# Turning x and the result in 32 x 32 blocks on VectorE instead of 128 x 128 tiles on TensorE

## The chip, the core and the metric

The kernel runs on one core of a Trainium2 chip. The metric is the device time of one execution in microseconds (us). The kernel before takes 1497.69 us, the median of 3 runs (1496.78 to 1500.61).

## What is computed

One layer of a streaming encoder, for 1024 prompt rows and 32 sample rows of 1024 features, all fp32. What matters here, cut from the reference:

```
h  = rms_norm(x, norm1_g) * (1 + sc1) + sh1
z  = h @ w_in                       # q, k, v, indexer, gMLP parts
attn = sparse attention over the top-k keys of each query; gm = gated MLP over chunks
y  = concat([attn, gm]) @ w_out
x  = x + g1 * y                     # x: the "residual"
h2 = rms_norm(x, norm2_g) * (1 + sc2) + sh2
x  = x + g2 * (square(relu(h2 @ w_ff1)) @ w_ff2)
return x, ...                       # y_prompt (1024 rows), y_sample (32 rows)
```

g1, g2, sc2 and sh2 have one value per feature, and differ between prompt and sample.

## The kernel before

From the product with w_out on, the kernel holds everything transposed: features on the 128 partitions, the 1056 rows (1024 prompt, then 32 sample) along the free dimension. A feature is then a partition, and the gates are one value per partition. The running x is kept in SBUF in eight blocks of 128 features, `xk(n, t0, n)`, each 128 x 1056; products are made in three chunks of 352 rows (`CW`, `NCK`). Each fp32 product is made of three passes over operands split in a high and a low part (`PASSES`), so a weight tile is first cast by ScalarE (L783) and its remainder taken by VectorE or GpSimd (L784).

Inputs and outputs in DRAM have rows of 1024 features, 4096 bytes. So x has to be turned twice:

- **In** (`x_col`, `x_chunk`, L755 to L769). For each feature block n, SyncE loads 128 columns of x into a buffer `xc` (two of them, tag XC): 1024 pieces of 512 bytes for the prompt and 32 for the sample. TensorE turns it in up to 128 x 128 tiles into PSUM (L768, 11 per block, the tiles being cut at the chunks' borders), and ScalarE copies each chunk to `xk` (L769). Blocks come in the groups (0, 1, 2), (3, 4), (5, 6, 7); for each group come x, then the weights (`wsplit`), then the products: for each chunk and block 24 matmuls (L839), whose sum VectorE multiplies by the gate and adds to `xk` in place (`gated`, L776). After the last group's chunk follows `norm2`.
- **Out** (`emit`, L867 to L882). The last part of `ff2` makes, for each feature block n and each chunk, 12 matmuls (L895) and adds the sum to `xk` (L776). When block n is done, TensorE turns it in nine tiles (L874), ScalarE copies them to a buffer `ot` (L876, L881), and SyncE stores it in pieces of 512 bytes (L879, L882). `ot` has one buffer for even n (tag OT) and shares the two buffers of XC for odd n. For the last block, n = 7, the store of the prompt is cut in two.

All transfers go through SyncE's queue, which issues them in order. The order of instructions on each engine is fixed when the kernel is built, by a planner that simulates a timeline; a buffer is given again when its last reader is done, for a store when it has landed.

Of the kernel before, what the change touches and what calls it, by code (L numbers as in the profile page):

```python
# [10 lines left out]
F32 = mybir.dt.float32  # L11
# [10 lines left out]
P = 128  # L22
D = 1024
KT = D // P
T = 1024
TS = 32
NT = T + TS
# [4 lines left out]
NB = T // P  # L32
# [6 lines left out]
CW = 352  # L39
NCK = 3  # L40
# [3 lines left out]
def blocks():  # L44
    return [(b, b * P, P) for b in range(NB)] + [(NB, T, TS)]
# [14 lines left out]
def hybrid_step(ctx: ExitStack, tc: tile.TileContext, i, o):  # L60
    nc = tc.nc
# [11 lines left out]
    def slot(shape, dt, name):  # L73
        return sp.tile(shape, dt, name=name, tag="S", bufs=15)
# [7 lines left out]
    def tp(name="tp"):  # L82
        return psz.tile([P, 512], F32, name=name, tag="C", bufs=2)
# [48 lines left out]
    ident = cst.tile([P, P], F32, name="ident")  # L132
# [71 lines left out]
    pt = tp("wst")  # L204
# [408 lines left out]
    key, c = {NB: sc_c[:, 384 + SD + 1024 + 256:].bitcast(I16)}, 0  # L613
# [112 lines left out]
    wf = phf.enter_context(tc.tile_pool(name="wf", bufs=1, reuse_waits="tile"))  # L726
    wn = phf.enter_context(tc.tile_pool(name="wn", bufs=1, reuse_waits="tile"))

    def mm(name="mm"):
        return psf.tile([P, 512], F32, name=name, tag="mm", bufs=6)  # L730
# [14 lines left out]
    def mix_at(k, c):  # L745
        return (gm[k - 4] if k >= 4 else attn[k])[:, :, c * CW:(c + 1) * CW]
# [3 lines left out]
    def xk(k, t0, n):  # L750
        if x2[k // 2] is None:
            x2[k // 2] = slot([P, 2, NT], F32, f"x2_{k}")
        return x2[k // 2][:, k % 2, t0:t0 + n]

    def x_col(n):  # L755

        x = wf.tile([P, NB + 1, P], F32, name="xc", tag="XC", bufs=2)
        nc.sync.dma_start(x[:, 0:NB, :], i["x_prompt"][0, :, n * P:(n + 1) * P].rearrange("(b p) c -> p b c", p=P))
        nc.sync.dma_start(x[:TS, NB, :], i["x_sample"][0, :, n * P:(n + 1) * P])
        return x  # L760

    def x_chunk(n, x, c):

        pt = tp("xt")
        for b, t0, m in blocks():
            a, e = max(t0, c * CW), min(t0 + m, (c + 1) * CW)
            if e > a:
                nc.tensor.transpose(pt[:, a - c * CW:e - c * CW], x[a - t0:e - t0, b, :], ident[a - t0:e - t0, a - t0:e - t0])  # L768
        nc.scalar.copy(xk(n, c * CW, CW), pt[:, :CW])  # L769


    def gated(part, k, c, ps):

        for s, a, n in spans(c):
            y = xk(k, c * CW + a, n)
            nc.vector.scalar_tensor_tensor(y, ps[:, a:a + n], mod[:, 8 * part + k, s:s + 1], y, op0=OP.mult, op1=OP.add)  # L776

    def wsplit(src, rearr, a, b, name, eng, extra=False):
        raw = rp.tile([P, a, b], F32, name=name + "r", tag="R4", bufs=2)
        nc.sync.dma_start(raw, src.rearrange(rearr, p=P))  # L780
        ws = wr.tile([P, 2, a, b], F32R, name=name, tag="E", bufs=1) if extra else wf.tile([P, 2, a, b], F32R, name=name, tag="W8", bufs=4)
        with tc.high_priority():
            nc.scalar.copy(ws[:, 0], raw)  # L783
        eng.tensor_tensor(ws[:, 1], raw, ws[:, 0].bitcast(F32), op=OP.subtract)  # L784
        return ws
# [8 lines left out]
    def norm2(c):  # L794

        acc = wn.tile([P, CW], F32, name="acc", tag="NA", bufs=3)
        for k in range(KT):
            x = xk(k, c * CW, CW)
            if k == 0:
                nc.scalar.activation(acc, x, AF.Square)  # L800
            else:
                sq = wn.tile([P, CW], F32, name="sq", tag="NS", bufs=3)
                nc.scalar.activation(sq, x, AF.Square)
                (nc.gpsimd if k < 7 else nc.vector).tensor_tensor(acc, acc, sq, op=OP.add)
        ps = tp("ssq")
        g = [(j, t, min(P, CW - t)) for j, t in enumerate(range(0, CW, P))]
        ms = small(4, "ms2")
        nc.gpsimd.memset(ms, 1.0)
        for j, t, m in g:
            nc.tensor.matmul(ps[:m, j:j + 1], acc[:, t:t + m], ones, start=True, stop=True)  # L810
        for j, t, m in g:
            nc.scalar.copy(ms[:m, j:j + 1], ps[:m, j:j + 1])
        r = rsqrt(ms, P, 4, "r2", D)
        y = tp("r2b")
        for j, t, m in g:
            nc.tensor.matmul(y[:, t:t + m], r[:m, j:j + 1].to_broadcast([m, P]), ident[:m, :m], start=True, stop=True)
        for k in range(KT):
            if (KT * c + k) % 3 == 0:
                h2.append(slot([P, 3, 2, CW], F32R, f"hh{c}_{k}"))
            hk = h2_at(k, c)  # L820
            f = wn.tile([P, CW], F32, name="hf2", tag="NH", bufs=2)
            for s, a, n in spans(c):
                nc.vector.scalar_tensor_tensor(f[:, a:a + n], xk(k, c * CW + a, n), a2[:, k, s:s + 1], y[:, a:a + n], op0=OP.mult, op1=OP.mult)
                nc.scalar.activation(hk[:, 0, a:a + n], f[:, a:a + n], AF.Identity, bias=mod[:, 24 + k, s:s + 1])
                nc.vector.scalar_tensor_tensor(hk[:, 1, a:a + n], f[:, a:a + n], mod[:, 24 + k, s:s + 1], hk[:, 0, a:a + n].bitcast(F32), op0=OP.add, op1=OP.subtract)  # L825

    KO = (4, 5, 6, 7, 0, 1, 2, 3)
    for ns in ((0, 1, 2), (3, 4), (5, 6, 7)):
        for n in ns:
            x = x_col(n)  # L830
            for c in range(NCK):
                x_chunk(n, x, c)
        ws = {n: wsplit(i["w_out"][0, :, n * P:(n + 1) * P], "(k p) c -> p k c", KT, P, "wo", nc.vector if n in (0, 2) else nc.gpsimd) for n in ns}
        for c in range(NCK):
            for n in ns:
                ps = mm("wo")
                for k in KO:
                    for q, (x, y) in enumerate(PASSES):
                        nc.tensor.matmul(ps[:, :CW], ws[n][:, x, k, :], mix_at(k, c)[:, y, :], start=k == KO[0] and q == 0, stop=k == KO[-1] and q == 2)  # L839
                gated(2, n, c, ps)  # L840
            if ns[-1] == KT - 1:
                norm2(c)
# [3 lines left out]
    NG = FF // (GH * P)  # L846
    phr.close()
    wr = phf.enter_context(tc.tile_pool(name="wr", bufs=1, side="right", reuse_waits="tile"))
# [15 lines left out]
                nc.gpsimd.tensor_tensor(hid[n][:, 1, c * CW:(c + 1) * CW], r, hi.bitcast(F32), op=OP.subtract)  # L864
        return hid

    def emit(n):  # L867

        ot = (wf if n % 2 else wr).tile([P, NB + 1, P], F32, name="ot", tag="XC" if n % 2 else "OT", bufs=2 if n % 2 else 1)
        for b0 in range(0, NB + 1, 4):  # L870
            pt = tp("yt")
            for b in range(b0, min(b0 + 4, NB + 1)):
                m = P if b < NB else TS
                nc.tensor.transpose(pt[:m, (b - b0) * P:(b - b0 + 1) * P], xk(n, b * P, m), ident)  # L874
            if b0 < NB:
                nc.scalar.copy(ot[:, b0:b0 + 4], pt.rearrange("p (b c) -> p b c", c=P))  # L876
                if n == KT - 1 or b0 == 4:
                    f0 = b0 if n == KT - 1 else 0
                    nc.sync.dma_start(o[0][0, f0 * P:(b0 + 4) * P, n * P:(n + 1) * P].rearrange("(b p) c -> p b c", p=P), ot[:, f0:b0 + 4])  # L879
            else:  # L880
                nc.scalar.copy(ot[:TS, NB, :], pt[:TS, :P])  # L881
                nc.sync.dma_start(o[1][0, :, n * P:(n + 1) * P], ot[:TS, NB, :])  # L882

    def ff2(gs):

        ks = [(g, k) for g in gs for k in range(GH)]
        for n4 in range(KT // 4):
            w = {g: wsplit(i["w_ff2"][0, g * GH * P:(g + 1) * GH * P, n4 * 512:(n4 + 1) * 512], "(k p) c -> p k c", GH, 512, "w2", nc.vector) for g in gs}
            for nn in range(4):
                n = 4 * n4 + nn  # L890
                for c in range(NCK):
                    ps = mm("f2")
                    for g, k in ks:
                        for q, (x, y) in enumerate(PASSES):
                            nc.tensor.matmul(ps[:, :CW], w[g][:, x, k, nn * P:(nn + 1) * P], hids[GH * g + k][:, y, c * CW:(c + 1) * CW], start=(g, k) == ks[0] and q == 0, stop=(g, k) == ks[-1] and q == 2)  # L895
                    gated(5, n, c, ps)
                if gs[-1] == NG - 1:
                    emit(n)

    hids = ff1((0, 1, 2))  # L900
    for g in range(NG - 1):
        if g:
            hids.update(ff1((2 * g + 2,)))
        if g < NG - 2:
            ff2([g])
        hids.update(ff1((2 * g + 3,)))
    ff2([NG - 2, NG - 1])
    phf.close()

# [35 lines left out]
```

## Time and profile before

| | us |
|---|---|
| median of 3 runs | 1497.69 |
| the profiled execution | 1491.26 |
| its span | 1489.5 |
| TensorE matmul busy in it | 1403.9 |
| VectorE / ScalarE / GpSimd busy | 821.7 / 549.2 / 551.0 |

The profile is of one execution, taken by the hardware profiler; times in it are from the start of its span. PE is TensorE's matmuls, PEld its weight loads, DVE VectorE, ACT ScalarE, POOL GpSimd, SP SyncE, which issues the transfers. The chain of waits is the work that ended last, followed back from the end: at each step to what released it.

### The profile page before, as it was taken

What the parts mean: (1) busy time and instruction counts of PE and PEld (TensorE: products, weight loads), DVE (VectorE), ACT (ScalarE), POOL (GpSimd) and SP (SyncE); (2) the same over time, 40 slices, a digit from 0 to 9 for tenths busy, and PEclk for the clock granted to TensorE, in tenths of its full rate; (3) what the DMA queues carried; (4) which work ended last, traced back from release to release, by engine and by line L of the source; (5) the groups of instructions that cost most, each with busy time, mean ns of one, the idle gap of its engine ahead of it and who ended that gap; (6) DMA issues with size and microseconds to landing.
All of it is one profiled execution on the core that took longest, in us unless ns stands there. A gap on an engine that the chain in (4) does not pass through costs nothing.

```text
span 1489.5 us, 23938 instructions
## 1 busy us (share of the span) xinstructions
PE 1403.9 (94%) x8952; PEld 1259.2 (85%) x8952; DVE 821.7 (55%) x1969; ACT 549.2 (37%) x1162; POOL 551.0 (37%) x831
## 2 busy tenths in 40 slices
PE   5889797887899999999999999999999999999998
PEld 1767576655567878899999999999999999999998
DVE  1689999998475867511673544335443344433422
ACT  2653356665545755522552212221122211122122
POOL 1646768667951433221342112221122211222120
PEclk9999899999899999999999999999999999999999
DMA  9221111256464221223111111111111111111113
GB/s 361 74 62 47 56 46 58 89 149 231 141 239 114 48 74 60 79 82 85 44 43 43 43 51 50 43 43 45 56 44 43 43 57 44 43 43 46 54 30 88
DMA packets 127611, 114.99 MB, mean 77 GB/s; under 512 B 24180, under 2 KB 95304, under 8 KB 126984
## 3 DMA queue, kind: packets, MB, share of 16 engines
q1 hardware_dynamic: 127496, 113.46, 24.8%
q8 instruction: 71, 1.16, 0.3%
q14 instruction: 44, 0.36, 0.1%
HBM read 97.97 MB, written 15.47 MB: 76 GB/s over the span
## 4 chain that ended last, share of the span: by engine, by line
PE 70%; DVE 16%; POOL 5%; issue 4%; ACT 3%; DMA 1%; SPq 0%; DVEq 0%; ACTq 0%; POOLq 0%
PE f L895 25%; PE f L858 23%; PE wo L839 6%; DVE tcjk L542 4%; PE pv L715 3%; PE lgp L690 3%; PE z L313 3%; PE ppt L702 3%; DVE tbjk L542 2%; PE xt L768 1%; POOL tasm L570 1%; DVE hh L825 1%; POOL wsp L195 1%; PE ada L154 1%; PE qst L360 1%
## 5 line engine op out<-in xcount | busy, mean ns | idle before, releaser
L895 PE MATMUL f<-hid,w 128*128 128x352 f32 x2304 | 377.3, 323 | 0.0
L858 PE MATMUL f<-hh,w 128*128 128x352 f32 x2304 | 372.3, 322 | 0.6 <-DVE hh L825 0.6
L858 PEld LDWEIGHTS f<-hh,w 128*128 128x128 f32 x2304 | 369.2, 188 | 0.9 <-DVE hh L825 0.9
L895 PEld LDWEIGHTS f<-hid,w 128*128 128x128 f32 x2304 | 369.3, 188 | 0.5
L776 DVE SCALAR_TENSOR_TENSOR x<-f,mod,x 128x352 f32<-128x352 f32 x480 | 222.4, 489 | 255.2 <-PE f L895 253.4
L313 PE MATMUL z<-wsp,h 128*128 128x512 f32 (+1 forms) x1152 | 284.9, 398 | 14.1 <-DVE ssh L424 4.6
L313 PEld LDWEIGHTS z<-wsp,h 128*128 128x128 f32 x1152 | 214.5, 198 | 72.2 <-issue 12.7
L863 POOL TENSOR_TENSOR rel<-rel 128x352 f32<-128x352 f32 x96 | 85.2, 889 | 512.6 <-ACT hid L862 512.6
L783 ACT CAST w<-w2r 128x1024 fp32r<-128x1024 f32 x32 | 33.6, 1049 | 285.7 <-PE f L895 272.7
L784 DVE TENSOR_TENSOR w<-w1r,w 128x1024 fp32r<-128x1024 f32 x32 | 40.6, 1267 | 138.0 <-ACT w L783 138.0
L860 ACT ACTIVATE rel<-f 128x352 f32<-128x352 f32 x96 | 44.3, 462 | 155.6 <-PE f L858 153.9
L864 POOL TENSOR_TENSOR hid<-rel,hid 128x352 fp32r<-128x352 f32 x96 | 91.3, 953 | 6.9
L695 POOL TENSOR_SCALAR lg<-lg,ast 128x128 f32<-128x128 f32 (+8 forms) x72 | 51.6, 719 | 97.1 <-DVE ast L694 73.9
L783 ACT CAST w<-w1r 128x1024 fp32r<-128x1024 f32 x32 | 33.5, 1047 | 85.7 <-PE f L858 73.3
L690 PE MATMUL lgp<-kst,qs 128*128 128x256 f32 (+1 forms) x336 | 61.0, 305 | 2.8 <-ACT qs L362 2.5
L195 POOL TENSOR_TENSOR wsp<-wraw,wsp 128x512 fp32r<-128x512 f32 (+1 forms) x44 | 55.0, 1262 | 16.9 <-ACT wsp L194 15.1
L784 DVE TENSOR_TENSOR w<-w2r,w 128x1024 fp32r<-128x1024 f32 x32 | 39.0, 1219 | 39.5 <-ACT w L783 39.5
L692 ACT ACTIVATE lg<-lg,ast 128x128 f32<-128x128 f32 (+8 forms) x72 | 53.9, 750 | 15.1 <-DVE ast L691 10.5
L542 DVE TENSOR_SCALAR_CACHE_REDUCE tcjk<-ya,tcsm 128x768 bf16<-128x768 int16 (+1 forms) x64 | 57.9, 942 | 0.9
L715 PE MATMUL pv<-pT,v 128*64 128x128 f32 (+2 forms) x624 | 57.7, 278 | 0.0
L776 DVE SCALAR_TENSOR_TENSOR x<-wo,mod,x 128x352 f32<-128x352 f32 (+2 forms) x32 | 15.1, 489 | 71.7 <-PE wo L839 71.7
L690 PEld LDWEIGHTS lgp<-kst,qs 128*128 128x128 f32 (+1 forms) x336 | 44.4, 186 | 11.1 <-issue 7.0
(349 smaller groups left out, 1839.5 us busy)
## 6 DMA issues: line engine op xcount, KB each, us to landing
wada<-in_w_ada_dram SPq DMA_DIRECT2D x24, 1024.0 KB, 6.0
w1r<-in_w_ff_dram SPq DMA_DIRECT2D x32, 512.0 KB, 4.0
w2r<-in_w_ff_dram SPq DMA_DIRECT2D x32, 512.0 KB, 3.8
wraw<-in_w_in_dram SPq DMA_DIRECT2D x40, 256.0 KB, 3.0
gm<-gmd SPq DMA_DIRECT2D x4, 1056.0 KB, 5.6
x<-in_x_prompt_dram SPq DMA_DIRECT2D x4, 1024.0 KB, 9.7
gmd<-gmt SPq DMA_DIRECT2D x8, 512.0 KB, 3.6
qn<-qd SPq DMA_DIRECT2D x8, 512.0 KB, 4.7
```

What stands on the lines that cost most here:

```text
L195: (nc.vector if c0 == CU and k % 2 else nc.gpsimd).tensor_tensor(ws[:, 1], raw, ws[:, 0].bitcast(F32), op=OP.subtract)
L313: nc.tensor.matmul(p[:m, :n], h[b][:, k, x, :], w[k][:, y, :], start=k == 0 and q == 0, stop=k == KT - 1 and q == 2)
L542: nc.vector.tensor_scalar(jk[:, :ncol[j]], src, val, None, op0=op, op1=OP.add, accum_out=cnt[:, j:j + 1])
L690: nc.tensor.matmul(ps[:m, d:d + kk.shape[1]], x, kk, start=q == 0, stop=q == 1)
L715: nc.tensor.matmul(ps[64 * j:64 * j + 64, :m], vv, pts[j][:w, k, :m], start=k == 0, stop=k == len(kts) - 1)
L776: nc.vector.scalar_tensor_tensor(y, ps[:, a:a + n], mod[:, 8 * part + k, s:s + 1], y, op0=OP.mult, op1=OP.add)
L784: eng.tensor_tensor(ws[:, 1], raw, ws[:, 0].bitcast(F32), op=OP.subtract)
L839: nc.tensor.matmul(ps[:, :CW], ws[n][:, x, k, :], mix_at(k, c)[:, y, :], start=k == KO[0] and q == 0, stop=k == KO[-1] and q == 2)
L858: nc.tensor.matmul(ps[:, :CW], ws[n][:, x, k, :], h2_at(k, c)[:, y, :], start=k == 0 and q == 0, stop=k == KT - 1 and q == 2)
L863: nc.gpsimd.tensor_tensor(r, r, r, op=OP.mult)
L864: nc.gpsimd.tensor_tensor(hid[n][:, 1, c * CW:(c + 1) * CW], r, hi.bitcast(F32), op=OP.subtract)
L895: nc.tensor.matmul(ps[:, :CW], w[g][:, x, k, nn * P:(nn + 1) * P], hids[GH * g + k][:, y, c * CW:(c + 1) * CW], start=(g, k) == ks[0] and ...
```

## The change

x and the result are turned by VectorE's transpose, which turns each 32 x 32 block of a tile in its place, and the transfers put the blocks where they belong. A quarter q of a feature block is 32 features on 32 partitions; a transfer places, for each group j of 32 rows, the 32 x 32 square of rows 32j to 32j+31 and the quarter's features, rows on partitions, in columns 32j to 32j+31. Each contiguous piece is 32 fp32, 128 bytes. One transpose of 128 x 1056 then gives the feature block. Per block there are 4 transfers for the prompt and 4 for the sample, in and out. The TensorE transposes and ScalarE copies of both places are dropped. Block n = 7 of the result is now turned and stored chunk by chunk, right after each chunk's sum; each of its three chunks takes a buffer of its own from tag XC.

```diff
--- before.py
+++ after.py
@@ -752,21 +752,20 @@
             x2[k // 2] = slot([P, 2, NT], F32, f"x2_{k}")
         return x2[k // 2][:, k % 2, t0:t0 + n]
 
-    def x_col(n):
-
-        x = wf.tile([P, NB + 1, P], F32, name="xc", tag="XC", bufs=2)
-        nc.sync.dma_start(x[:, 0:NB, :], i["x_prompt"][0, :, n * P:(n + 1) * P].rearrange("(b p) c -> p b c", p=P))
-        nc.sync.dma_start(x[:TS, NB, :], i["x_sample"][0, :, n * P:(n + 1) * P])
-        return x
-
-    def x_chunk(n, x, c):
-
-        pt = tp("xt")
-        for b, t0, m in blocks():
-            a, e = max(t0, c * CW), min(t0 + m, (c + 1) * CW)
-            if e > a:
-                nc.tensor.transpose(pt[:, a - c * CW:e - c * CW], x[a - t0:e - t0, b, :], ident[a - t0:e - t0, a - t0:e - t0])
-        nc.scalar.copy(xk(n, c * CW, CW), pt[:, :CW])
+    def squares(t, n):
+
+        return [t[:, n * P + 32 * q:n * P + 32 * q + 32].rearrange("(j a) b -> a j b", a=32) for q in range(4)]
+
+    def quarter(t, q):
+        return t[32 * q:32 * q + 32].rearrange("a (j b) -> a j b", b=32)
+
+    def x_rows(n):
+
+        x = wf.tile([P, NT], F32, name="xc", tag="XC", bufs=2)
+        for t, src in ((x[:, 0:T], i["x_prompt"][0]), (x[:, T:NT], i["x_sample"][0])):
+            for q, s in enumerate(squares(src, n)):
+                nc.sync.dma_start(quarter(t, q), s)
+        nc.vector.transpose(xk(n, 0, NT), x)
 
 
     def gated(part, k, c, ps):
@@ -827,9 +826,7 @@
     KO = (4, 5, 6, 7, 0, 1, 2, 3)
     for ns in ((0, 1, 2), (3, 4), (5, 6, 7)):
         for n in ns:
-            x = x_col(n)
-            for c in range(NCK):
-                x_chunk(n, x, c)
+            x_rows(n)
         ws = {n: wsplit(i["w_out"][0, :, n * P:(n + 1) * P], "(k p) c -> p k c", KT, P, "wo", nc.vector if n in (0, 2) else nc.gpsimd) for n in ns}
         for c in range(NCK):
             for n in ns:
@@ -864,22 +861,15 @@
                 nc.gpsimd.tensor_tensor(hid[n][:, 1, c * CW:(c + 1) * CW], r, hi.bitcast(F32), op=OP.subtract)
         return hid
 
-    def emit(n):
-
-        ot = (wf if n % 2 else wr).tile([P, NB + 1, P], F32, name="ot", tag="XC" if n % 2 else "OT", bufs=2 if n % 2 else 1)
-        for b0 in range(0, NB + 1, 4):
-            pt = tp("yt")
-            for b in range(b0, min(b0 + 4, NB + 1)):
-                m = P if b < NB else TS
-                nc.tensor.transpose(pt[:m, (b - b0) * P:(b - b0 + 1) * P], xk(n, b * P, m), ident)
-            if b0 < NB:
-                nc.scalar.copy(ot[:, b0:b0 + 4], pt.rearrange("p (b c) -> p b c", c=P))
-                if n == KT - 1 or b0 == 4:
-                    f0 = b0 if n == KT - 1 else 0
-                    nc.sync.dma_start(o[0][0, f0 * P:(b0 + 4) * P, n * P:(n + 1) * P].rearrange("(b p) c -> p b c", p=P), ot[:, f0:b0 + 4])
-            else:
-                nc.scalar.copy(ot[:TS, NB, :], pt[:TS, :P])
-                nc.sync.dma_start(o[1][0, :, n * P:(n + 1) * P], ot[:TS, NB, :])
+    def emit(n, c=None):
+
+        t0, t1 = (0, NT) if c is None else (c * CW, (c + 1) * CW)
+        ot = (wf if n % 2 else wr).tile([P, NT], F32, name="ot", tag="XC" if n % 2 else "OT", bufs=2 if n % 2 else 1)[:, :t1 - t0]
+        nc.vector.transpose(ot, xk(n, t0, t1 - t0))
+        parts = [(ot[:, :min(t1, T) - t0], o[0][0, t0:min(t1, T)])] + ([(ot[:, T - t0:], o[1][0])] if t1 > T else [])
+        for src, dst in parts:
+            for q, d in enumerate(squares(dst, n)):
+                nc.sync.dma_start(d, quarter(src, q))
 
     def ff2(gs):
 
@@ -894,7 +884,9 @@
                         for q, (x, y) in enumerate(PASSES):
                             nc.tensor.matmul(ps[:, :CW], w[g][:, x, k, nn * P:(nn + 1) * P], hids[GH * g + k][:, y, c * CW:(c + 1) * CW], start=(g, k) == ks[0] and q == 0, stop=(g, k) == ks[-1] and q == 2)
                     gated(5, n, c, ps)
-                if gs[-1] == NG - 1:
+                    if gs[-1] == NG - 1 and n == KT - 1:
+                        emit(n, c)
+                if gs[-1] == NG - 1 and n < KT - 1:
                     emit(n)
 
     hids = ff1((0, 1, 2))
```

## Rows read from the trace of the kernel before

**Rows 1.** The page: busy time of each engine; the chain's shares by engine

```profile
PE 1403.9 (94%) x8952; PEld 1259.2 (85%) x8952; DVE 821.7 (55%) x1969; ACT 549.2 (37%) x1162; POOL 551.0 (37%) x831
...
PE 70%; DVE 16%; POOL 5%; issue 4%; ACT 3%; DMA 1%; SPq 0%; DVEq 0%; ACTq 0%; POOLq 0%
```

**Rows 2.** Busy time by stretch: its ends and length, engines, clock, DMA share

```profile
core 0: us, PE busy (x) PEld busy (x) DVE busy (x) ACT busy (x) POOL busy (x), PEclk, DMA share, GB/s
623.70:713.40 89.70, 89.70 (x538) 82.08 (x538) 14.44 (x28) 23.51 (x46) 21.53 (x14) 1.00 0.32 90
713.40:765.40 52.00, 51.44 (x333) 51.15 (x331) 42.23 (x94) 30.20 (x71) 17.21 (x18) 1.00 0.14 41
765.40:1430.70 665.30, 665.25 (x4153) 665.25 (x4154) 274.46 (x506) 144.39 (x238) 168.81 (x184) 1.00 0.15 46
1430.70:1484.10 53.40, 53.40 (x354) 52.52 (x354) 15.39 (x31) 11.70 (x24) 1.86 (x2) 1.00 0.25 69
1484.10:1489.50 5.40, 1.29 (x9) 0.71 (x7) 0.71 (x2) 1.32 (x3) 0.00 (x0) 0.96 0.49 132
```

**Rows 3.** The chain from 620 to 720 us, in order: start, length, what

```profile
by line: PE wo L839 80.8%; PE xt L768 15.0%; PE pv L715 2.7%; PE ppt L702 1.2%; PE ssq L810 0.5%
...
623.77 1.20 PE xt L768 x7
...
712.14 0.75 PE xt L768 x4
```

**Rows 4.** The chain from 1430 to 1490 us

```profile
by line: PE f L895 77.3%; PE yt L874 12.4%; PE f L858 1.6%; ACT ot L876 1.0%; DVE x L776 0.9%; ACTq L941 0.2%; issue 0.2%
...
1437.12 0.22 PE yt L874 x2
...
1482.98 1.13 PE f L895 x7
...
1484.13 0.56 DVE x L776
...
1484.74 0.56 PE yt L874 x3
...
1485.32 0.58 ACT ot L876
```

**Rows 5.** VectorE on fp32 by shape, busy, mean ns; last min/median/max ns

```profile
L241 DVE TENSOR_SCALAR x<-x,rxy 128x1024 f32<-128x1024 f32 x8 | 6.8, 877 | 0.1
L784 DVE TENSOR_TENSOR w<-w1r,w 128x1024 fp32r<-128x1024 f32 x32 | 40.6, 1267 | 138.0 <-ACT w L783 138.0
L804 DVE TENSOR_TENSOR acc<-acc,sq x3: 510/519/524, 711.3 to 740.1; 128x352 f32<-128x352 f32 x3
```

**Rows 6.** DMA, 291 to 294 us, a 128-byte store (40 slices; packets, MB, share)

```profile
GB/s 0 0 0 0 0 0 0 0 0 0 0 0 0 0 0 0 0 0 75 123 109 109 109 109 109 108 109 109 109 109 109 109 109 108 24 0 0 0 0 0
...
q1 hardware_dynamic: 1040, 0.13, 33.6%
```

**Rows 7.** DMA, 1461 to 1467.75 us, a block's 512-byte store

```profile
q1 hardware_dynamic: 1088, 0.54, 29.0%
```

**Rows 8.** DMA, 520 to 540 us, a load in 256-byte pieces

```profile
q1 hardware_dynamic: 2064, 0.52, 11.7%
```

**Rows 9.** SyncE's issues in order of time: start, length, line, what

```profile
607.44 0.38 SPq L758 DMA_DIRECT2D xc<-in_x_prompt_dram  x1
...
608.95 0.84 SPq L759 DMA_DIRECT2D xc<-in_x_sample_dram  x1
...
623.77 2.61 SPq L780 DMA_DIRECT2D wor<-in_w_out_dram  x2
...
1486.40 0.50 SPq L882 DMA_DIRECT2D out_dram<-ot  x1
```

**Rows 10.** The sample's stores, L882: issue min/median/max ns; issue to landing

```profile
L882 SPq DMA_DIRECT2D out_dram<-ot x8: 332/332/570, 1443.8 to 1486.4; - x8
...
DMA to landing us min/median/max: 2.0/2.2/3.0
```

## The prediction

> **What bounds the kernel now.** Read the page's busy shares and chain of waits first: TensorE is busy for 94% of the span and holds 70% of the chain that ended last [rows 1]. The share is an average, so the next view is the table by stage [rows 2]. From 623.7 to 1484.1 us TensorE idles for 0.6 us altogether, nearly all of it in 713 to 765 us, while VectorE has 14.4 of 89.7 us, 42.2 of 52.0 us and 15.4 of 53.4 us of work in the three stages that the change touches or borders on. [...] Then the chain, cut to the two places: it runs through every transpose of x [rows 3] and through the transposes of the result [rows 4]. After the last matmul TensorE is done and the chain is VectorE, three transposes, a ScalarE copy and the stores: 5.4 us from 1484.1 to the end.
>
> **TensorE's transposes of x.** 88 transposes go, in 18 pieces of the chain, the first and the last of which stand in [rows 3]; the pieces add up to 15.0 us, the 15.0% that the head of this 100 us cut gives. Matmuls stand on both sides of each piece and wait for nothing, so all of it comes off: **-15.0 us**. The 24 ScalarE copies that go with them cover nothing and are worth nothing.
>
> What is late next? x must now be landed and turned by VectorE before the first product of that column block is added to it. Loads: per block 4 transfers of 1024 packets and 4 of 32, 264 packets per DMA engine instead of 66. No load of 128-byte packets is in the trace. The nearest row is a store of 1040 such packets: 131 KB at a flat 109 GB/s is 1.20 us, 18.8 ns a packet on each of 16 engines [rows 6]. The other bound is the 512-byte packet, 0.290 x 6.75 us x 16 / 1088 = 28.8 ns [rows 7]; a 256-byte load comes to 0.117 x 20 us x 16 / 2064 = 18.1 ns of engine time [rows 8]. I take 18.8: 5.0 us a block, at most 7.6. SyncE issues four transfers in 1.5 us, so 0.5 us apiece [rows 9]: 64 issues instead of 16, 32 us of queue in some 105 us. The first two blocks can start at 607.4 us, as now [rows 9], and are there at about 613.5 and 618.5 us (616 and 624 at the upper bound). A block's 24 matmuls of 161 ns [rows 4] take 3.9 us, so the first product is added at 627.6 us and the third block's at 635.4 us. The third block's load starts when the first has been turned (about 615 us) and is landed by 624, or 632 at the upper bound. All are in time.
>
> VectorE's transpose is not in the trace. From below: the 128 x 1024 scalar operation on fp32, 0.88 us. From above: one pass at 1.27 us for each of the four groups of 32 partitions, 5.1 us. By the nearest row, a 128 x 1024 two-input fp32 operation of 1.27 us [rows 5], 1056 columns take 1.3 us, which I take; 352 columns take 0.52 us, as in the 128 x 352 row [rows 5]. Eight times 1.3 is 10 us beside the 14.4 of 89.7 us, hidden; even 8 x 5.1 = 41 us fits there. [...]
>
> VectorE's queue is in order: behind a transpose that waits for its load stand attention's last evictions and the splits of w_out, and TensorE waits for those. Behind x's issues on SyncE stands the third w_out load, which goes out at 623.8 us when its buffer is free [rows 9]. If all is placed after the data this costs nothing; I take nothing and keep 8 us as the other end (rival 1).
>
> The stage from 713 to 765 us, where VectorE is nearly full, gets no new work: all eight blocks of x are turned before it. Its start moves up with TensorE's, so the 0.6 us idle stays.
>
> **TensorE's transposes of the result.** Seventy-two, 7.5 us of the chain in 30 pieces; the last 0.56 us comes after the last matmul [rows 4]. **-6.9 us** ahead of that point: the 53.4 us stage becomes 46.5, 5.8 us a block. Against it, per block: VectorE 15.4 / 8 + 1.3 = 3.2 us, 7.0 at the upper bound; SyncE 8 issues of 0.5 us, 4.0; the rings 264 x 18.8 ns = 5.0 us where now 66 packets at 28.8 ns need 1.9. All below 5.8, the rings with 14% to spare: **this is where the change can fail** (rival 2). An even block's buffer is needed again two blocks, 11.6 us, after its own transpose; its stores are landed after some 6 us.
>
> [...]
>
> **The end.** Times here are from the last matmul's end. Now: stores are issued until 1486.4, the last lands 2.2 us later, and 0.9 us follow to the span's end [rows 9, 10], +5.4. After: block 6 is added up at -5.8 + 0.6 and turned by -3.9; its 8 issues last to +0.1. Packets start 0.75 us after an issue and run from -3.15 to +1.8. Block 7 comes in three chunks. The first (352 columns, 88 packets an engine, 1.65 us) is issued to 2.1, moved by 3.5 and landed at 3.8; the second is issued to 4.1. The third has the first chunk's buffer (two of them, in turn), so its transpose waits for 3.8, not for its sum at 0.6, and ends at 4.35. Eight issues follow (four of the prompt, four of the sample); the last starts at 7.85, lands 2.2 us later and is followed by 0.9 us: +10.95. **+5.5 us**. Without the buffer's wait it would be 0.25 less, since SyncE is busy to 4.1 anyway. If the issues took the 0.33 us of the sample's store [rows 10] apiece, with no gap, some 1.2 us less.
>
> **Sum.** -15.0 - 6.9 + 5.5 = -16.4 us. The profiled execution took 1491.26 us (span 1489.5 and 1.8 around it), so 1474.9 for the same. The median of the runs is 1497.69, 6.4 us above that execution; the difference is carried over: **1481 us**, with its own range 1475 to 1488.
>
> **Rivals.**
> 1. *x or w_out come late at the start.* Place: SyncE's queue at 615 to 630 us. If the fifth block's x is put ahead of the third w_out load, its eight issues wait for a buffer and take 4 us themselves, and the load with its split is some 5 us late, once in the first group and at most once more: 3 to 8 us of TensorE idle, 1484 to 1489. For it: order on a queue is fixed beforehand, on guessed transfer times. Against it: x is first wanted a whole block later than now.
> 2. *The stores bind: slower.* Place: the rings from the first result on. Above 5.8 us / 264 = 22 ns a packet, each block's stores last longer than its matmuls, the buffers come back late and TensorE waits. The stores begin at -46.5 + 5.8 + 0.6 + 1.3 + 0.75 = -38 and need 8 x 264 packets, so the end is -36.8 + 2.11 per ns. At 28.8 ns that is +24, 18.6 above now's: 21.9 - 18.6 leaves 3.3 us, 1494. From 30.4 ns it is slower; at twice the row's price, 37.6 ns, the end is +42.5 and the time is 1497.7 + 15.2 = 1513. For it: the one row of 128 bytes is a single short store, from 128 partitions at a pitch of 4224 bytes, where this one reads 32 partitions and writes at 4096. Against it: the 512-byte stores now write at that very pitch at full rate.
> 3. *The first saving doesn't arrive.* If the VectorE work of 713 to 765 us stays where it is, only -6.9 + 5.5 = -1.4 is left: 1496. For it: 42 of 52 us busy there. Against it: that work hangs on sums that move up.
> 4. *VectorE binds.* At 5.1 us a transpose the result's stage needs 7.0 us a block, 1.2 x 8 us back and 1.2 more in the last chunk, 10.8: 1492.
>
> **How the numbers follow.** Forecast 60%; rival 1, 15%; rival 2 slower than before 9%, and in its part from 22 to 30 ns 6%; rival 3, 5%; rival 4, 3%; a reordering elsewhere 2%. Below 0.3%, 4.5 us, a measurement here can't tell a change from none. Faster by more than that: the forecast, rival 1, rival 4 and a part of rival 2's milder half, 80%. The same: the other part, rival 3 and some of the reordering, 10%. Slower: 10%. The range goes from 1474 (an end no longer than now gives 1476, and small gains between matmuls) to 1495, rival 2 at 28.8 ns.
>
> **What would show it.** Right: no transposes in the chain after 620 us; the products with w_out within 75 us in place of 89.7; the result's stage at 46.5 us with TensorE full; transposes of 1.3 us; 18 to 20 ns a packet; an end of some 11 us. Wrong: VectorE's transposes or TensorE waiting for a load before 640 us (rival 1); transposes of the result waiting for their buffer before the last block, DMA rows full throughout (rival 2); a stall at the first product with w_ff1 well over 0.6 us (rival 3).

## The result, and the profile after

The changed kernel takes 1483.93 us in the median (1477.36 to 1490.53, 8 runs) against 1497.24 us (1488.86 to 1500.61, 8 runs): a ratio of 0.9936, 95% interval 0.9909 to 0.9963. It is faster by 0.6%, the interval lying below 1; the median is 2.9 us above the forecast of 1481 and inside the range. The profiled execution went from 1491.26 to 1479.71 us, by 11.5 us; the forecast for it was 16.4. These 4.9 us are what there is to explain.

The page of the changed kernel, busy times and the chain's shares, answers to [rows 1]:

```profile
PE 1380.9 (93%) x8792; PEld 1244.5 (84%) x8792; DVE 843.5 (57%) x1987; ACT 528.8 (36%) x1114; POOL 550.0 (37%) x831
...
PE 68%; DVE 17%; POOL 5%; issue 4%; SPq 3%; ACT 2%; DMA 2%; DVEq 0%; POOLq 0%; ACTq 0%
```

The 160 transposes are gone (8952 to 8792 TensorE instructions), and SyncE's sequencer, SPq, has come into the chain with 3%. Next the table by stage of the changed kernel, columns as in [rows 2], cut where TensorE ends attention and begins the products with w_out, begins those with w_ff1, begins the last 288 products, behind which the eight blocks of the result are stored, and ends its last matmul:

```profile
623.86:725.06 101.20, 96.09 (x596) 95.81 (x595) 39.86 (x68) 25.08 (x48) 31.16 (x23) 0.98 0.45 85
725.06:1419.05 693.99, 693.99 (x4341) 693.97 (x4340) 303.14 (x569) 163.32 (x281) 175.28 (x191) 1.00 0.15 46
1419.05:1465.47 46.42, 46.42 (x289) 46.13 (x288) 24.66 (x40) 1.91 (x3) 1.86 (x2) 1.00 0.53 77
1465.47:1478.00 12.53, 0.00 (x0) 0.00 (x0) 1.26 (x3) 0.00 (x0) 0.00 (x0) 0.66 0.45 65
```

The kernel before, cut at the same two points ahead of the result's stage; its w_out stage begins with the first transpose of x, at 623.70:

```profile
623.70:735.74 112.04, 112.04 (x684) 104.42 (x683) 30.46 (x63) 34.93 (x72) 31.63 (x23) 1.00 0.27 77
735.74:1430.69 694.95, 694.34 (x4341) 694.04 (x4339) 300.66 (x565) 163.17 (x281) 175.91 (x191) 1.00 0.15 46
```

| stage | before, us | after, us | difference | forecast |
|---|---|---|---|---|
| start to w_out's stage | 623.70 | 623.86 | +0.2 | 0 |
| w_out's stage | 112.04 | 101.20 | -10.8 | -15.0 |
| w_ff's products | 694.95 | 693.99 | -1.0 | 0 |
| the result's stage [rows 2] | 53.40 | 46.42 | -7.0 | -6.9 |
| after the last matmul [rows 2] | 5.40 | 12.53 | +7.1 | +5.5 |

The result's stage came out as forecast. Two rows did not: w_out's stage, in which TensorE now idles for 101.20 - 96.09 = 5.1 us, and the end.

**The stall in w_out's stage.** The waits of the changed kernel from 600 to 765 us (us in all, times, longest):

```profile
DVE x L768 <- DMA xc<-in_x_sample_dram: 19.4, 6, 6.9
...
PE wo L836 <- ACT wo L782: 5.1, 1, 5.1
```

TensorE waits once, for a split of w_out. VectorE waits much longer for x, but no wait of TensorE comes from that. SyncE's issues (start, length, count of transfers) show why the split is late:

```profile
614.63 3.65 SPq L767 DMA_DIRECT2D xc<-in_x_sample_dram  x4
625.95 3.40 SPq L767 DMA_DIRECT2D xc<-in_x_prompt_dram  x4
629.40 2.22 SPq L767 DMA_DIRECT2D xc<-in_x_sample_dram  x4
631.71 0.39 SPq L779 DMA_DIRECT2D wor<-in_w_out_dram  x1
```

The third w_out load went out at 623.77 [rows 9]; now it goes out at 631.71. In front of it stands the third block of x: eight issues, which first wait until a buffer is free. VectorE shows when that is:

```profile
624.27 0.29 DVE L718 TENSOR_TENSOR attn<-pv,attn 128x128 fp32r<-128x128 f32 x1 [0.37 <-ACT attn L717]
624.65 1.28 DVE L768 STREAM_TRANSPOSE x<-xc 128x1056 f32<-128x1056 f32 x1
```

The first transpose of x runs at 624.65, behind attention's last eviction, although the last of its block's loads was issued by 612.3. So the buffer comes free at 625.93, the queue moves on at 625.95, and the chain of waits then leads straight to TensorE:

```profile
624.65 1.29 DVE x L768
...
629.40 0.83 SPq L767
631.71 4.03 DMA wor<-in_w_out_dram
635.82 1.05 ACT wo L782
636.91 68.46 PE wo L836 x416
```

The load itself is not slow: it takes 4.03 us from its issue, where w_out's loads of 620 to 640 us in the kernel before landed after 3.8.

The idle costs more than itself. The stretches of 4 us around it:

```profile
628.00:632.00 4.00, 3.81 (x24) 3.52 (x22) 1.93 (x3) 0.50 (x1) 0.00 (x0) 1.00 0.61 92
632.00:636.00 4.00, 0.00 (x0) 0.00 (x0) 1.71 (x2) 0.68 (x2) 0.93 (x1) 1.00 0.94 193
636.00:640.00 4.00, 3.08 (x11) 3.09 (x12) 1.23 (x1) 0.86 (x1) 0.00 (x0) 0.57 0.93 91
640.00:644.00 4.00, 4.00 (x27) 4.00 (x27) 1.28 (x1) 0.00 (x0) 0.00 (x0) 1.00 0.85 119
```

After the idle the granted clock is 0.57 for a stretch: 11 matmuls take 3.08 us where 27 take 4.00 in the next row, so about 3.08 - 11 x 4.00 / 27 = 1.45 us are lost.

**The end.** The chain from 1460 us on, its larger pieces: VectorE's transposes of block 6 and of the last block's first piece, SyncE's issues, a landing, the last transpose:

```profile
1460.47 1.28 DVE ot L868
...
1462.97 0.56 SPq L872
...
1464.29 0.92 SPq L872
...
1465.26 1.50 SPq L872
...
1467.74 0.42 SPq L872
...
1469.68 1.76 DMA out_dram<-ot
...
1471.67 0.55 DVE ot L868
```

Against the last matmul's end at 1465.47, block 6 is turned at -3.7 (forecast -3.9). But its eight issues begin only at -2.9, behind those of block 5, and last to +2.7 (forecast: -3.9 to +0.1): 5.6 us, 0.70 apiece. The sixteen issues of block 7 take 0.49 apiece, as forecast. All that follows block 6 is later by its delay: the first piece lands at +6.0 (forecast +3.8), the last transpose ends at +6.75 (+4.35), the last issue begins at +10.2 (+7.85). The three pieces of block 7 take XC's two buffers in turn, so the last piece waits for the first one's store; they do not have a buffer each. All stores and transposes of the result in the changed kernel (min/median/max ns, first and last start):

```profile
L872 SPq DMA_DIRECT2D out_dram<-ot x72: 355/464/1710, 1429.2 to 1475.7; - x72
L868 DVE STREAM_TRANSPOSE ot<-x x10: 545/1278/1279, 1427.9 to 1471.7; 128x1056 f32<-128x1056 f32 x7, 128x352 f32<-128x352 f32 x3
```

### The profile page after: what moved, and what is told of

Read it like the earlier page. It is cut to its first block, busy times and chain, and to the rows that moved or that the text cites. A ratio compares the mean times of both kernels' runs of the same rounds, so it can differ in the third digit from the quotient of the medians.

```text
span 1478.0 us, 23705 instructions
## 1 busy us (share of the span) xinstructions
PE 1380.9 (93%) x8792; PEld 1244.5 (84%) x8792; DVE 843.5 (57%) x1987; ACT 528.8 (36%) x1114; POOL 550.0 (37%) x831
## 4 chain that ended last, share of the span: by engine, by line
PE 68%; DVE 17%; POOL 5%; issue 4%; SPq 3%; ACT 2%; DMA 2%; DVEq 0%; POOLq 0%; ACTq 0%
PE f L855 25%; PE f L885 22%; PE wo L836 6%; DVE tcjk L542 4%; PE pv L715 3%; PE lgp L690 3%; PE z L313 3%; PE ppt L702 3%; DVE tbjk L542 2%; SPq L872 2%; POOL tdsm L571 1%; PE ada L154 1%; DVE tcsm L582 1%; DVE sc_b L379 1%; PE qst L360 1%
## 5 line engine op out<-in xcount | busy, mean ns | idle before, releaser
L885 PE MATMUL f<-hid,w 128*128 128x352 f32 x2304 | 372.0, 322 | 0.0
L775 DVE SCALAR_TENSOR_TENSOR x<-f,mod,x 128x352 f32<-128x352 f32 (+1 forms) x480 | 222.2, 489 | 238.3 <-PE f L885 236.7
L836 PE MATMUL wo<-gm,wo 128*128 128x352 f32 x288 | 51.9, 329 | 5.1 <-ACT wo L782 5.1
```

## The experiments

Runs differ by up to 11 us before the stage that the change touches: with the same code there the first product with w_out began at 623.9 us in the changed kernel's profile and at 634.2 in e4's, where the mean granted clock of the run was 0.974 and 0.959. So profiles are compared by the time from the start of w_out's stage to the end of the span, *the tail* below, in kernels where TensorE turns x from its first transpose of x: 1489.5 - 623.7 = 865.8 us before, 1478.0 - 623.86 = 854.1 after. Ratios are to the kernel before, on the same chip.

**The two halves.** First theory: the order on SyncE's queue costs w_out's stage some 6.6 us, and the new end takes all that the result's stage gains. Its rival: the small packets themselves, of loads and stores, slow the w_out loads and TensorE's work. e1 loads x in the new way and has the old result; e2 the reverse.

```diff
 e1, against the changed kernel
-    def emit(n, c=None):      # nc.vector.transpose, 128-byte stores
+    def emit(n):              # yt transposes on TensorE, as before
 e2, against the changed kernel
-            x_rows(n)
+            x = x_col(n)      # xt transposes on TensorE, as before
+            for c in range(NCK):
+                x_chunk(n, x, c)
```

> x is turned by VectorE, the result by TensorE as before. Theory A (each side pays by itself: x's side takes 15 us of transposes off TensorE and gives 5 back while the third w_out load waits behind x's issues; the result's side takes 7.0 us off and gives 7.1 back in the end): the span is that of the changed kernel, 1478 us give or take 1, TensorE idle for 5 us at about 632 us, 5.4 us from the last matmul to the end. Rival (the result's side earns part of the gain): 1480 or more, by as much as that side earns.

> x is turned by TensorE as before, the result by VectorE. Theory A: nothing is gained, span 1489.5 us give or take 1, the last stage 7.0 us shorter and the end 12.5 instead of 5.4 us; the ratio to before holds 1.0. Rival (the end is long only because all of the change is there, or the stores cost less than the transposes did): 1483 to 1487.

e1: 1485.43 us (1477.66 to 1490.01, 10 runs) against 1492.66, ratio 0.9936 (0.9910 to 0.9962), tail 855.6. It has the stall, and a granted clock of 0.50 behind it (its waits, and the stretch of 4 us after the idle):

```profile
PE wo L836 <- ACT wo L782: 5.9, 1, 5.9
```

```profile
644.00:648.00 4.00, 3.39 (x11) 3.39 (x12) 1.54 (x2) 0.56 (x1) 0.00 (x0) 0.50 0.86 99
```

e2: 1497.07 us (1489.59 to 1501.83, 10 runs), ratio 1.0023 (1.0002 to 1.0044), tail 866.7, 0.9 longer than before. All of the gain is x's; the result's half gives nothing, and with this end its interval lies just above 1. The spans themselves (1486.4 and 1492.2) missed what was expected, since their w_out stages began at 630.8 and 625.5 us.

**w_out ahead of x.** If the order on the queue is the cause, w_out's loads written first must take the wait away with the same packets; if the packets are, it must stay.

```diff
+        ws = {n: wsplit(i["w_out"]...) for n in ns}
         for n in ns:
             x_rows(n)
-        ws = {n: wsplit(i["w_out"]...) for n in ns}
```

> As the changed kernel, but each group's w_out loads stand ahead of its x loads in the program, so that the third w_out load is ahead of the second and third block's x on SyncE's queue. Theory A (order on the queue makes that load late): TensorE idles for under 0.5 us from 624 to 700 us and the span is 5 us shorter, 1473. Rival B (128-byte packets fill the DMA rings and any load among them is late): the load lands 8 us or more after its issue, the idle of 5 us stays within 1 us, span 1477 to 1478.

1477.65 us (1470.19 to 1480.95, 4 runs), ratio 0.9897 (0.9864 to 0.9929), tail 847.0, 7.1 below the changed kernel's. The third load goes out as the stage begins, and the stage has no idle time left:

```profile
629.05 0.39 SPq L779 DMA_DIRECT2D wor<-in_w_out_dram  x1
```

```profile
629.00:723.50 94.50, 94.50 (x595) 94.50 (x595) 39.36 (x68) 25.08 (x48) 31.49 (x23) 1.00 0.50 97
```

The order is the cause: among the same packets the wait of 5.1 us is gone once the load goes out ahead of them, and in e3 the last loads of x's first block are issued as late as 629.48 to 630.52 us without a wait of TensorE. The stage takes 101.2, 102.8, 101.7 and 102.7 us in the four profiles of the changed order (the changed kernel, e1, e4, e9) and 94.5 in each of three with w_out first (e3, e10, e11).

And 112.04 - 94.50 = 17.5 us are gone where the transposes in the chain were 15.0: the products' own busy time fell too. By form of w_out's products in the kernel before, then in e3:

```profile
L839 PE MATMUL wo<-attn,wo 128*128 128x352 f32 x288 | 53.2, 327 | 0.0
```

```profile
L836 PE MATMUL wo<-attn,wo 128*128 128x352 f32 x288 | 50.6, 323 | 0.0
```

The other half of these products, on gm, went from 51.7 to 50.5 us; together 3.8, of which 2.5 show in the stage's length. Away from transposes twelve products take 1.92 to 1.95 us in both kernels, so these 2.5 us lie at the changes between transposes and products, 0.14 us at each of the 18 pieces.

**The end: buffer, queue or packets.** Three theories: the last piece waits for its buffer (the forecast's own step); one queue issues too slowly; the 128-byte packets are too slow. e4 gives each of the last block's pieces a buffer of its own:

```diff
-        ot = (wf if n % 2 else wr).tile(...)[:, :t1 - t0]
+        if c is None:
+            ot = (wf if n % 2 else wr).tile(...)
+        else:
+            ot = wn.tile([P, CW], F32, name="ot", tag="NS", bufs=3)
```

> As the changed kernel, but the three chunks of the last result block have buffers of their own, so that no transpose waits for a store. Theory A (the end is SyncE's row of 24 issues from the seventh block on): the last transpose comes 5 us earlier, but its stores still queue behind the issues; the end is 0.2 to 1 us shorter, 11.5 to 12.3 us after the last matmul. Rival C (the wait for the buffer sets the end): 4 to 5.5 us shorter, 7 to 8.5 us after the last matmul.

One run, 1490.08 us; tail 854.2, end 12.1 us instead of 12.5. Taking the wait away gives 0.4 us at most, for the changed kernel's own end was 12.2 in e9: behind the buffer stands the queue. (The stall at w_out, 5.5 us, is in this kernel too.) e5 has w_out first, as e3, and lets ScalarE's queue issue every second store:

```diff
-                nc.sync.dma_start(d, quarter(src, q))
+                (nc.scalar if q % 2 else nc.sync).dma_start(d, quarter(src, q))
```

> w_out loads first, as in the third experiment, and the stores of the second and fourth quarter are issued by ScalarE, the others by SyncE. Theory A (SyncE's row of issues sets the end): the end is 3 to 5 us shorter, 7.5 to 9 us after the last matmul, the ratio to before 0.987. Rival D (the DMA rings set it, and SyncE's issues are long only because the rings are full): the end stays within 1.5 us of 12.1 us, each queue's issues get longer.

1476.27 us (1475.51 to 1477.16, 4 runs) against 1495.57, ratio 0.9882 (0.9850 to 0.9914); the end is 8.7 us against e3's 12.1. The stores by queue:

```profile
L872 SPq DMA_DIRECT2D out_dram<-ot x36: 315/563/1532, 1427.9 to 1470.1; - x36
L872 ACTq DMA_DIRECT2D out_dram<-ot x36: 334/679/1549, 1427.9 to 1470.2; - x36
```

An issue is longer (medians 0.56 and 0.68 us, 0.46 in the changed kernel), as the third theory has it, but two run at a time. The eight issues of a block begin 5.5 to 5.9 us after those of the block before in the changed kernel, and are out after some 3.9 us in e5. The busy tenths of the DMA engines from 1426 to 1438 us, in 40 slices, for e3 and then e5:

```profile
DMA  0000000049999879999961100108999989999985
DMA  0000000003999987999998418999978999987100
```

With one queue the engines are nearly idle for six slices between two blocks, while the last short issues go out; with two the next block follows almost at once, and the engines are mostly 0.7 to 0.9 busy. So both of the last two theories hold a part. e6 has w_out first and stores the last block whole, in 8 transfers in place of 16:

```diff
-                    if gs[-1] == NG - 1 and n == KT - 1:
-                        emit(n, c)
-                if gs[-1] == NG - 1 and n < KT - 1:
+                if gs[-1] == NG - 1:
```

> w_out loads first; the last result block is turned and stored in one piece like the others, 8 issues instead of 16, but nothing of it before its last sum. Theory A: the eight issues start at 2.7 us after the last matmul, when those of the block before are done, the last lands at about 9, the end is 9.5 to 10.5 us after the last matmul, against 12.1. Rival E (storing chunk by chunk shortens the end, as the block's first two thirds are out earlier): 13 us or more.

One run, 1476.33 us, an end of 9.25 us: the last block in pieces, meant to store earlier, costs 2.8 us; its 16 issues took 7.8 us in the changed kernel, the 8 of e6 take 5.3. e7 joins w_out first, own buffers and two queues:

> w_out loads first, stores issued by ScalarE and SyncE in turn, and buffers of their own for the last block's three chunks. Theory A: the last chunk's stores follow its sum at once, end 6 to 7.5 us after the last matmul, span 4.5 to 6 us under the third experiment's for the same start of the w_out stage, ratio to before 0.986. Rival D: an end of 10 us or more.

1472.57 us (1468.24 to 1472.80, 4 runs), ratio 0.9848 (0.9819 to 0.9878); the end is 7.95 us, a little more than expected, and the tail 842.9, 4.1 under e3's where 4.5 to 6 were expected. The last transpose no longer waits for a store but follows the last sum, at +0.8:

```profile
1462.55 0.03 issue
1462.58 0.72 DVE x L775 x2
1463.30 0.02 issue
1463.32 0.55 DVE ot L871
```

**Every store twice.** To measure the cost of the stores themselves, e8 is e3 with each store issued twice, with the same data.

```diff
                 nc.sync.dma_start(d, quarter(src, q))
+                nc.sync.dma_start(d, quarter(src, q))
```

> w_out loads first; every store of the result is issued twice, to the same place. Each block then has 16 issues and twice the packets. Theory A (one block's stores take some 5 of the 5.8 us that its matmuls take): they take 10 us now and bind; the result's stage is 70 to 85 us in place of 46.3, TensorE waits for VectorE's sums behind transposes that wait for a buffer, span 28 to 45 us longer. Rival (stores have much room): the stage stays at 46 to 50 us and only the end gets longer, by 5 to 8 us.

One run, 1526.45 us, tail 891.3, 44.3 us above e3. The size fell where it was expected, the place did not: TensorE is full for 46.6 us and never waits; VectorE waits for buffers, and the whole delay lies in an end of 56.4 us. The waits from 1420 us on, the two lines of stores, and the two stretches:

```profile
DVE ot L868 <- DMA out_dram<-ot: 48.6, 6, 14.4
```

```profile
L872 SPq DMA_DIRECT2D out_dram<-ot x72: 328/559/1615, 1432.0 to 1521.0; - x72
L873 SPq DMA_DIRECT2D out_dram<-ot x72: 315/431/992, 1434.6 to 1522.5; - x72
```

```profile
1421.70:1468.30 46.60, 46.59 (x291) 46.30 (x289) 19.77 (x33) 1.91 (x3) 1.86 (x2) 1.00 0.55 80
1468.30:1524.70 56.40, 0.00 (x0) 0.00 (x0) 5.62 (x12) 0.00 (x0) 0.00 (x0) 0.54 0.61 88
```

144 issues fill SyncE's queue from 1432.0 to 1522.5, 0.63 us apiece, while the DMA engines are busy for 0.61 of the last stretch. So the queue binds, though not by its issues alone: in the changed kernel an issue takes 0.37 us with the engines' share at 0.04 (1434.71) and up to 1.71 behind the packets of its block (1442.85); that the packets hold it up is read from where the long ones fall, and not tested alone. There a block's eight issues, 5.5 to 5.9 us, already filled the 5.8 that its matmuls take.

**Once more, on one chip.** The changed kernel, e3 and e7 again, sharing 14 runs of the kernel before (1495.26 us).

> The changed kernel once more, on the same chip as the next two. Both theories: w_out's stage 101 us with TensorE idle for some 5 us, an end of 12.5 us, ratio to the kernel before about 0.993. It is the base for the next two.

> w_out's loads ahead of x in the program, as in the earlier run, now beside the changed kernel. If the order on SyncE's queue costs the changed kernel 5.1 us of idle time and some 1.5 us of half clock, this one is 5 to 8 us shorter than it in the medians (ratio to before about 0.988). If the earlier difference of the medians came from the chip, the two are within 3 us.

> w_out first, own buffers for the last block's pieces and two issuing queues, beside the other two. By the traces: 4 us shorter than with w_out first alone and 11 us shorter than the changed kernel (ratio to before about 0.985). If ScalarE's share of the issues delayed its other work, less than 2 us shorter than with w_out first alone.

| | median, us (runs) | ratio, 95% | tail, us | end, us |
|---|---|---|---|---|
| changed | 1482.18 (9) | 0.9931 (0.9904 to 0.9957) | 855.4 | 12.2 |
| w_out first | 1478.98 (6) | 0.9896 (0.9869 to 0.9923) | 847.6 | 12.7 |
| all three edits | 1471.77 (6) | 0.9841 (0.9811 to 0.9871) | 842.8 | 7.9 |

The tails repeat within 1.3 us and differ by 7.8 and 4.8 us. The medians agree for all edits (10.4 below the changed kernel) but show 3.2 us for w_out first, where 5 to 8 were expected, and the intervals of these two overlap a little; with the runs' spread ahead of the tail (the means of the same runs differ by 6.0), 3.2 is no contradiction, but the size of that step rests on the traces. The version with all three edits beats both kernels.

## Why the prediction was right, and where it was not

- *TensorE's transposes of x, -15.0*: right in kind, small in size. They cost 2.5 us more at the changes to the matmuls beside them, 17.5 in all (e3).
- ***The step that failed*: "The third block's load starts when the first has been turned (about 615 us)... I take nothing."** The load of x had been timed, the transpose that frees its buffer had not: on VectorE it stands behind attention's last eviction and runs at 624.65. The third block's issues then kept SyncE from the third w_out load for 7.9 us; TensorE idled for 5.1 us, and the granted clock of 0.57 behind the idle cost about 1.5 more. This is rival 1 in its place, by its own sign (TensorE waiting before 640 us) and at its price (6.6 us in its 3 to 8), but with the third block of x and not the fifth, and in every profile of this order (e1, e4, e9). Its chance of 15% was too low: the prediction named the in-order queue and a full buffer in front of a load that TensorE needs, and set against it only when x is wanted, which is not what the queue goes by. Why the order by which instructions were laid out puts that first transpose so late is open.
- *The 0.6 us before w_ff1, "stays"*: it went, with 0.4 more, -1.0.
- *TensorE's transposes of the result, -6.9*: -7.0.
- *The end, +5.5*: +7.1. Mis-sized term: "SyncE 8 issues of 0.5 us". In block 6 they took 0.70 apiece and began 0.8 us late, the queue being full (0.63 on average in e8). The wait of the last piece for its buffer, which the forecast priced at 0.25 us, was worth 0.4 at most (e4).
- *Packets at 18.8 ns, the stores with 14% to spare*: cheaper. The DMA engines' busy tenths and rate while two blocks' stores run, 1446 to 1458 us of the changed kernel (40 slices):

```profile
DMA  0106999988999996201005999987999996210010
GB/s 11 13 0 100 144 145 144 133 122 109 163 170 151 146 135 86 27 2 14 10 4 78 143 143 144 143 128 92 168 168 175 137 148 95 26 16 8 6 14 3
```

  A plateau of 143 GB/s is 131 KB in 0.92 us, 14.3 ns a packet on each of 16 engines, and the low slices between blocks (27 down to 2) are the slack. Rival 2 was far off by packets alone; by the queue, whose eight issues took 5.5 to 5.9 us against the 5.8 of a block's matmuls, it was near. Four such packets cost 4 x 14.3 / 28.8 = 2.0 times one of 512 bytes [rows 7], where the 18.8 ns of the forecast come to 2.6.
- *VectorE's transpose, 1.3 and 0.52 us*: 1.278 and 0.545. The 704 columns between the two forms take 733 ns, 1.04 ns each; at that price 352 columns are 0.37 us, so by this estimate from the two forms 0.18 us of each instruction does not go with its columns. Rival 4, at 5.1 us a transpose, is out; rival 3 too, since w_out's and w_ff's stages kept their gain.

The sum again, from the forecast: -16.4 + 5.1 + 1.5 (stall and clock) - 2.5 (matmuls beside the transposes) - 1.0 (w_ff) - 0.1 + 1.6 (end) + 0.2 (start) = -11.6, against -11.5 measured. That the forecast came so near is in part luck: 8.4 us that it lacked were offset by 3.6 of gains that it had not priced, and the median came nearer still (2.9 us) because the changed kernel's lies 4.2 us above its profiled run where the forecast carried over 6.4. Measured at 1483.93, the kernel lies at the edge of rival 1's 1484 to 1489.

## What to carry to other kernels

Work taken off a full engine paid in full only where what replaced it did not stand in a queue that the engine depends on (17.5 us of w_out's stage in e3, 10.8 in the changed kernel): for each in-order queue, list what is behind the new transfers, and time the instruction that frees their buffer, not only the data that it needs. Many small transfers are paid in issues as well as in packets: on one queue the two added up to 5.5 to 5.9 us a block here, on two to 3.9. Count both against one queue under load, and give a second queue its share. At the end of this kernel, on one queue, storing the last block in pieces cost 2.8 us more than storing it whole (e6, 9.25 against 12.1 us).

## What the runs showed that was not expected

After 5.1 us without a matmul the granted clock of the next stretch of 4 us was 0.57 in the changed kernel (0.50 after 5.9 us in e1), and of the one behind it 1.00 (0.83 in e1). So idle time and clock together cost 6.7 us of w_out's stage in the changed kernel's profile and 8.3 in e1's. In e9, whose stage has 5.5 us without a matmul, the longest product of the stage took 659 ns where the median is 323. Taking out 88 transposes gave 2.5 us of stage more than their own pieces of the chain. A second queue did not double the rate of 128-byte stores: its issues were longer, and a block was out in 3.9 us where one queue took 5.5, with the DMA engines mostly 0.7 to 0.9 busy.
